# Load order, the order of a plain product's column halves, and the engine of the first block's remainders in a one-core decoder trunk kernel

## The chip, the cores and the metric

The kernel runs on one core of one Trainium2 chip. The core has TensorE (PE, matrix products, with the weight loads PEld beside them), VectorE (DVE), ScalarE (ACT), GpSimd (POOL) and SyncE (SP), which issues most of the transfers; each has an instruction queue of its own that it works through in order. The metric is the device time of one execution in microseconds, less is better. The kernel before takes 968.28 us, the median of three runs.

## What is computed

One layer of a decoder trunk over 1024 tokens and 16 meta tokens of width 1024. The root-mean-square norm of the tokens goes through one wide projection `w_in`, and its columns are shared out among four mixers (pooling, latent attention, a convolution module, a short gated convolution) and their gates; the four results are gated, projected, added, projected once more and normalised. This document is about the start only: the norm and the first columns of the projection.

```python
h = rms_norm(h_res, pre_norm_g[i])          # h_res: 16 meta tokens, then 1024 tokens
z = h @ w_in[i]
(pv, pg, cq, ckv, kr, mg, cu, cg, sbcx, sg, gl) = split_cols(z)
y_b = (mla_attention(cq, ckv, kr, ...) * jax.nn.silu(mg)) @ w_out_mla[i]
y_c = (conformer_conv(cu, ...) * jax.nn.silu(cg)) @ w_out_conf[i]
```

## The kernel before

**Precision.** Every fp32 operand of a product is kept as two parts, a rounded one ("hi") and the remainder ("lo"). A product is then three matmuls: hi by hi, hi weight by lo data, lo weight by hi data. `split` (line 497) makes the two: ACT copies the rounded part, another engine subtracts it from the source. Unless it is told otherwise that is POOL.

**Tokens and blocks.** The 1024 tokens are eight tiles of 128, x0 to x7. Transposed, with the 1024 rows of the projection in two halves, they make four blocks of data: B11 and B21 from x0 to x3 (first and second half of the rows), B12 and B22 from x4 to x7. The 16 meta tokens (`xm`) become columns 512 to 527 of B11 and B21. The projection is done with 7 products of sums and differences of blocks in place of 8. So there are four more operands: T1, T2, T4 from the differences of x tiles t and t + 4, and T3, which shares its buffer's name with B12. On the weights' side a block of 512 rows by 128 columns gives A11, A12, A22 and the sums S1 to S4. `prep` (line 592) loads two raw blocks, forms the sums on DVE and makes the seven pairs of hi and lo with `blk`. `unit` (line 633) runs the seven products for one range of columns of the tokens, into four PSUM banks.

**The plain product.** The columns `ckv` and `kr` (128 and 32 wide) are needed first and are not done with the sums. `plain` (line 678) runs, for one range of columns, four products of the raw weights: for the first half of the tokens (x0 to x3: `ckv` into bank pa, `kr` into pb), then for the second half (x4 to x7). It is called for the ranges U0 (columns 0 to 255, that is tiles 0, 1 and 4, 5) and U1 (columns 256 to 527: tiles 2, 3 and the meta tokens, and columns 256 to 511 of the second half: tiles 6, 7). All four need hi and lo of their data in both halves of the rows.

**One tile's way.** `load_x` issues the load on SP. `square` sums the squares (ACT, with a table function that accumulates), POOL forms the reciprocal root of the mean in two small instructions (`rsqrt_mean`, tile `rsx`), DVE multiplies the tile by it and by the gain (`scaled`, two halves of 512), PE transposes each half in four 128x128 pieces into a PSUM bank (`operand_of`, two banks x and one y in turn), ACT copies the rounded part, DVE subtracts to get the remainder. `parts` does this for the tiles that it is given, with one reciprocal root for all of them. `sums_of(t)` then forms four differences of tiles t and t + 4 on POOL, in place, and makes T1, T2 and T4 from them.

**What sets the order.** The program is not issued as written. A planner (`Plan`) records every operation, with an estimated length and its dependencies, and then emits each engine's operations in the order that its own clock gives. Operations inside `plan.ahead` come earlier than their place. When PE has nothing ready the planner puts in up to eight transposes of the identity in a row (tile `ps_w`), which nothing reads; they stop after the first block. Tiles come from small rings, so an operation may also wait for the buffer of an earlier one: the seven buffers `blk` hold x1 to x3, the meta tokens and the plain weights first, then the first block's weights.

**Order around the change.** The loads go out as x0, x1, x4, x5, the two raw blocks of the plain weights (`raw_kv`, 320 KB each), x2, x6, x3, x7, meta tokens; an x tile has 512 KB. The calls are `parts(0)`, `parts(1)`, the splits of the plain weights, `parts(4, 5)`, `parts(2, 6)`, `parts(3, 7)`, `meta()`, then `plain` for U0, the sums of tiles 0 and 1, `prep` of the first block, the sums of 2 and 3 and `plain` for U1.

Of the kernel before, what the change touches and what calls it, by code (L numbers as in the profile page):

```python
# [23 lines left out]
BF16 = mybir.dt.bfloat16  # L24
AF = mybir.ActivationFunctionType
ALU = mybir.AluOpType
# [4 lines left out]
P = 128  # L31
D = 1024
# [21 lines left out]
C_CU, C_CG, C_SC, C_SG, C_GL = 1440, 1952, 2208, 2976, 3232  # L54
# [8 lines left out]
B11, B21, B22, T1, T2, T3, T4 = range(7)  # L63

B12 = T3
# [6 lines left out]
def f(ap):  # L72
    return ap.bitcast(F32)
# [397 lines left out]
def trunk_kernel(ctx, tc, a):  # L471
    nc = tc.nc
    plan = Plan(nc)
    PE, ACT, DVE, POOL, SP = (plan.engine(e) for e in ("PE", "ACT", "DVE", "POOL", "SP"))
    ctx.enter_context(tc.manual_schedule())

    def pool(stack, grain=64, **kw):
        return plan.open(stack, Pool(plan, stack.enter_context(tc.tile_pool(bufs=1, **kw)), grain=grain,
                                     psum=kw.get("space") == PSUM,
                                     side="dram" if kw.get("space") == DRAM else kw.get("side", "left")))  # L480
# [4 lines left out]
    def copy(out, in_, scale=1.0):  # L485
        ACT.activation(out, in_, AF.Copy, scale=scale)

    def sub(eng, out, x, y):
        eng.tensor_tensor(out, x, y, op=ALU.subtract)

    def add(eng, out, x, y):
        eng.tensor_tensor(out, x, y, op=ALU.add)
# [4 lines left out]
    def split(hi, lo, src, eng=None):  # L497
        copy(hi, src)
        sub(eng or POOL, lo, src, f(hi))
# [12 lines left out]
    def rsqrt_mean(out, ssq, n, eps=EPS, eng=DVE):  # L512

        eng.tensor_scalar(out, ssq, 1.0 / n, eps, op0=ALU.mult, op1=ALU.add)
        POOL.tensor_tensor(out, out, mhalf[:out.shape[0], :out.shape[1]], op=ALU.pow)
# [43 lines left out]
    def bank(tag="x"):  # L559

        return psum.tile([P, 512], F32, tag=tag, bufs=2 if tag == "x" else 1, name=f"ps_{tag}")
# [3 lines left out]
    tp = pool(one, name="tp", reuse_waits="tile")  # L565
# [3 lines left out]
    def t4(shape, dt=F32, name="t4"):  # L569
        return tp.tile(shape, dt, tag="t4", bufs=4, name=name)  # L570
# [12 lines left out]
    def raw(name):  # L583

        return wp.tile([P, KH, 2 * P], F32, tag="raw", bufs=3, name=name)

    def blk(src, name):
        b = wp.tile([P, 2, KH, P], F32R, tag="blk", bufs=7, name=name)
        split(b[:, 0], b[:, 1], src)
        return b  # L590

    def prep(c):

        (a11, a21), (a12, a22) = ((t[:, :, :P], t[:, :, P:]) for t in (wload(0, c), wload(1, c)))
        ss = raw("ss")
        s1, s2 = ss[:, :, :P], ss[:, :, P:]
        add(DVE, s1, a21, a22)  # L600
        sub(DVE, s2, s1, a11)
        sub(DVE, a21, a11, a21)
        w = {n: blk(src, n) for n, src in (("A11", a11), ("S2", s2), ("S1", s1), ("S3", a21))}
        sub(DVE, s2, a12, s2)
        w.update({n: blk(src, n) for n, src in (("A12", a12), ("A22", a22), ("S4", s2))})
        return w

    def product(ps, w, b, c0, n, start, stop):
# [66 lines left out]
            out(0, 1, pc, u2[:, :nb], u2)  # L675
        pump()

    def plain(w, c0, n, out):

        for j, bs in enumerate(((B11, B21), (B12, B22))):  # L680
            for i, m in enumerate((P, 64)):
                ps = bank(("pa", "pb")[i])[:m, :n if j == 0 else min(n, 512 - c0)]
                for h, b in enumerate(bs):
                    (product, stacked)[i](ps, w[h][i], b, c0, n, h == 0, h == 1)
                with plan.ahead(EVAC):
                    out(i, j, ps, None, None)
# [35 lines left out]
    def out_raw(names, c0, n):  # L722

        z, place = pairs_of(n)

        def out(i, j, ps, x, tmp):
            second = i in z
            full(place(i, j, ps), x, ps)
            if second:
                store_both(names[i], z[i][:ps.shape[0]], c0, n)  # L730
        return out
# [60 lines left out]
    def wload(i, c, n=2 * P):  # L792

        t = raw("raw")
        for e, c_ in enumerate(c if isinstance(c, tuple) else (c,)):
            m = P if isinstance(c, tuple) else n
            SP.dma_start(t[:, :, P * e:P * e + m], w_in[:, KH * i:KH * (i + 1), c_:c_ + m])
        return t

    xt = {}  # L800

    def load_x(t):

        xt[t] = (t4([P, D], name="x") if t in (4, 5, 6, 7) else
                 wp.tile([P, D], F32, tag="raw", bufs=3, name="x") if t == 0 else
                 wp.tile([P, D], F32, tag="blk", bufs=7, name="x"))
        for c in (slice(0, 512), slice(512, D)) if t == 0 else (slice(0, D),):
            SP.dma_start(xt[t][:, c], a["x"][0, P * t:P * (t + 1), c])
    g8 = tp.tile([KD, P], F32, tag="wraw", bufs=2, name="g8")

    with plan.slow(-2000):
        load_x(0)
        ACT.dma_start(g8, a["pre_norm_g"][0].rearrange("(k p) -> k p", p=P))
        load_x(1)
        load_x(4)
        load_x(5)
        raw_kv = [wload(i, C_CKV, P + 32) for i in range(2)]
        for t in (2, 6, 3, 7):
            load_x(t)
        xm = wp.tile([NM, D], F32, tag="blk", bufs=7, name="xm")  # L820
        SP.dma_start(xm, a["meta_tokens"])
# [8 lines left out]
    ssx = const.tile([P, 16], F32, name="ssx")  # L830
    rsx = const.tile([P, 16], F32, name="rsx")

    def square(x_, t):
        n = x_.shape[0]
        ACT.activation(tp.tile([P, D], BF16, tag="whl", name="junk")[:n], x_, AF.Square, accum_out=ssx[:n, t:t + 1])

    def scaled(x_, t):
        n = x_.shape[0]
        for i in range(2):
            s = slice(512 * i, 512 * (i + 1))  # L840
            DVE.scalar_tensor_tensor(x_[:, s], x_[:, s], rsx[:n, t:t + 1], gB[i][:n], op0=ALU.mult, op1=ALU.mult)
# [3 lines left out]
    def operand_of(b, t, src):  # L845

        turn[0] += 1
        pt = bank("xxy"[turn[0] % 3])
        for k in range(KH):
            PE.transpose(pt[:, P * k:P * (k + 1)], src[:, P * k:P * (k + 1)], ident)  # L850
        p3 = pt.rearrange("p (k n) -> p k n", n=P)
        c = slice(P * t, P * (t + 1))
        copy(HB[b][:, 0, :, c], p3)
        sub(DVE, HB[b][:, 1, :, c], p3, f(HB[b][:, 0, :, c]))

    def parts(*ts):

        r0 = turn[1]
        turn[1] += len(ts)
        for i, t in enumerate(ts):  # L860
            square(xt[t], r0 + i)
        rsqrt_mean(rsx[:, r0:r0 + len(ts)], ssx[:, r0:r0 + len(ts)], D, eng=POOL)
        for i, t in enumerate(ts):
            scaled(xt[t], r0 + i)
            for j, b in enumerate(((B11, B21), (B12, B22))[t // 4]):
                operand_of(b, t % 4, xt[t][:, 512 * j:512 * (j + 1)])

    def sums_of(t):

        (b11, b21), (b12, b22) = ((xt[i][:, :512], xt[i][:, 512:]) for i in (t, t + 4))  # L870
        sub(POOL, b11, b12, b11)
        sub(POOL, b12, b22, b12)
        sub(POOL, b22, b22, b11)
        sub(POOL, b21, b21, b22)
        for b, src in ((T1, b11), (T2, b22), (T4, b21)):
            operand_of(b, t, src)

    def meta():
        square(xm, 8)
        rsqrt_mean(rsx[:NM, 8:9], ssx[:NM, 8:9], D, eng=POOL)  # L880
        scaled(xm, 8)
        pt = bank()
        for k in range(KD):
            PE.transpose(pt[:, NM * k:NM * (k + 1)], xm[:, P * k:P * (k + 1)], ident[:NM, :NM])
        b1, b2 = (pt[:, 64 * i:64 * (i + 1)].rearrange("p (k n) -> p k n", n=NM) for i in range(2))
        hm = up.tile([P, 2, KH, NM], F32, tag="u2", name="hm")
        copy(hm[:, 0], b1)
        sub(DVE, hm[:, 1], b2, hm[:, 0])
        for b, src, eng in ((B11, b1, DVE), (B21, b2, DVE), (T2, b1, DVE), (T4, hm[:, 1], DVE)):
            split(HB[b][:, 0, :, 512:LH], HB[b][:, 1, :, 512:LH], src, eng)  # L890
# [12 lines left out]
    U0, U1 = (0, 256), (256, 256 + NM)  # L903
# [6 lines left out]
    w_kv = [[blk(t[:, :, :P], "kv")] for t in raw_kv]  # L910
    kr = wp.tile([P, 2, KH, 64], F32R, tag="blk", bufs=7, name="kr")
    for i, t in enumerate(raw_kv):
        split(kr[:, i, :, :32], kr[:, i, :, 32:], t[:, :, P:P + 32])
        w_kv[i].append(kr[:, i])
    parts(4, 5)
    out_kv = [out_raw(("ckv", "kr"), *u) for u in (U0, U1)]
    parts(2, 6)
    parts(3, 7)
    meta()
    plain(w_kv, *U0, out_kv[0])  # L920
    for t in range(2):
        sums_of(t)
    w = prep((C_CU, C_CU + 256))
    for t in range(2):
        operand_of(T3, t, xt[t + 4][:, :512])
    for t in range(2, 4):
        sums_of(t)
    plain(w_kv, *U1, out_kv[1])
    for t in range(2, 4):
        operand_of(T3, t, xt[t + 4][:, :512])  # L930
    prow = w1([P, P], name="prow")
# [530 lines left out]
    for i, (_, names, kind) in enumerate(pairs):  # L1462
# [11 lines left out]
        w = nxt  # L1474
# [381 lines left out]
    for d in (0, 4, 1, 5, 2, 6, 3, 7):  # L1856
        whl = [wtile(ep, "w_out_mla", d, i) for i in range(2)]
        th = ep.tile([P, NT], F32, tag="th", bufs=3, name="th")
        ld(th, th_dram[8 + d])
        for c in range(2):  # L1860
            t = th[:, 512 * c:512 * (c + 1)]
            py = bank("u")
            for k in range(4):
                b = boM[c][k]
                w = whl[k // 2][:, :, k % 2]
# [154 lines left out]
```

## Time and profile before

| | before |
|---|---|
| median of three runs | 968.28 us (965.73 to 969.6) |
| the profiled execution | 959.63 us |
| its span, first to last instruction | 957.9 us |
| mean granted TensorE clock | 0.997 |
| data moved | 205.96 MB, mean 215 GB/s |
| instructions | 15219 |

The profiled execution has its own time; the span leaves out 1.7 us around the instructions. Nearly all instructions are recorded by one helper and carry line 361, so rows are told apart by their tiles: `ps_pa<-B,kv` is a matmul into bank pa of the operand B with the weights kv. In a timeline a row holds the start, the length, the engine, the operation, out<-in with sizes, how many of them follow one another, and in brackets the idle time before them with what ended it. PE's lengths overlap, since matmuls are pipelined; the distance between two starts is what a row occupies. The first 33 us, up to the meta tokens, are the stage in which the tiles are normalised and transposed; the first block's `unit` follows the plain product.

The fullest rows of what engines wait for in the first 60 us (waiter, waited for, us in total, times, longest):

```profile
POOL rsx L361 <- ACT junk L361: 7.6, 3, 4.0
DVE x L361 <- POOL rsx L361: 4.6, 3, 2.5
ACT z L361 <- DVE z L361: 4.1, 2, 3.6
DVE u L361 <- PE ps_pb L361: 3.7, 2, 2.5
ACT junk L361 <- DMA x<-in_x_dram: 3.0, 3, 1.5
```

### The profile page before, as it was taken

Reading aid. Unit: us, or ns where it says so; the run is one execution under the profiler, and the core shown is the slowest. Engines: PE = TensorE matmul, PEld = TensorE weight load, DVE = VectorE, ACT = ScalarE, POOL = GpSimd, SP = SyncE. Lnnn points to the kernel's source line nnn. Section 1 sums busy time; section 2 is a strip of 40 time slices with the busy share of each in tenths; the row PEclk is TensorE's granted clock in tenths of the full one; section 3 lists DMA queues with packets and bytes.
Section 4 is the critical chain, followed back from the end, with each engine's and each line's share of the span. In section 5 each row is a group of like instructions: output and inputs, shape, how many; then the busy total and the mean of one; then the engine's idle time right before and its main releaser. Section 6 shows DMA issues by size and latency. Waiting matters only on the chain.

```text
span 957.9 us, 15219 instructions
## 1 busy us (share of the span) xinstructions
PE 943.9 (99%) x4945; PEld 804.2 (84%) x4945; DVE 720.2 (75%) x1124; ACT 453.5 (47%) x925; POOL 677.7 (71%) x627
## 2 busy tenths in 40 slices
PE   8999999999999999999999999999999999999996
PEld 8998999988888888888888888888878878788885
DVE  6856979996999799547583657337778888799857
ACT  7752343434444445544454543266556565225632
POOL 5957669668787768669775977466467686738955
PEclk9999999999999999999999999999999999999998
DMA  8146566676779886788686678798978663783543
GB/s 262 46 126 198 151 202 196 211 224 204 249 229 280 281 283 209 244 224 245 221 255 187 191 243 279 220 300 259 294 207 275 199 184 111 264 266 107 189 141 144
DMA packets 143876, 205.96 MB, mean 215 GB/s; under 512 B 21169, under 2 KB 88752, under 8 KB 143028
## 3 DMA queue, kind: packets, MB, share of 16 engines
q1 hardware_dynamic: 134820, 188.20, 63.9%
q10 hardware_dynamic: 8656, 15.74, 4.5%
q8 instruction: 39, 0.64, 0.3%
q0 software_dynamic: 320, 1.05, 0.3%
q14 instruction: 41, 0.34, 0.1%
HBM read 132.01 MB, written 72.89 MB: 214 GB/s over the span
## 4 chain that ended last, share of the span: by engine, by line
PE 92%; DVE 3%; POOL 2%; issue 1%; ACT 1%; DMA 1%; SPq 0%; DVEq 0%; POOLq 0%; ACTq 0%
PE ps_pa L361 17%; PE ps_pb L361 17%; PE ps_pc L361 16%; PE ps_o L361 9%; PE ps_pd L361 8%; PE ps_u L361 7%; PE ps_s L361 7%; PE ps_y L361 6%; PE ps_x L361 4%; DMA x<-in_x_dram 1%; DVE th L361 1%; POOL pt L361 0%; ACT junk L361 0%; DVE op L361 0%; DVE c L361 0%
## 5 line engine op out<-in xcount | busy, mean ns | idle before, releaser
L361 PE MATMUL ps_pa<-B,A 128*128 128x512 f32 (+2 forms) x792 | 171.9, 359 | 0.0
L361 PE MATMUL ps_pb<-T,S 128*128 128x512 f32 (+2 forms) x792 | 170.7, 358 | 0.2 <-DVE u L361 0.2
L361 PEld LDWEIGHTS ps_pb<-T,S 128*128 128x128 f32 x792 | 134.4, 189 | 22.4 <-DVE u L361 0.4
L361 PEld LDWEIGHTS ps_pa<-B,A 128*128 128x128 f32 x792 | 134.2, 188 | 21.2 <-issue 0.2
L361 POOL TENSOR_TENSOR S<-ss,S 128x512 fp32r<-128x512 f32 x84 | 116.4, 1398 | 50.1 <-ACT S L361 43.3
L361 POOL TENSOR_TENSOR pt<-p,pt 128x512 fp32r<-128x512 f32 (+1 forms) x96 | 102.2, 1089 | 53.3 <-PE ps_s L361 27.4
L361 POOL TENSOR_TENSOR A<-raw,A 128x512 fp32r<-128x512 f32 x84 | 114.3, 1370 | 36.0 <-ACT A L361 35.7
L361 DVE TENSOR_TENSOR u<-ps_pb,u 128x512 f32<-128x512 f32 (+2 forms) x66 | 40.2, 610 | 67.3 <-PE ps_pb L361 62.2
L361 DVE SCALAR_TENSOR_TENSOR ps_w<-conv,par,ps_w 128x512 f32<-128x512 f32 x116 | 87.2, 752 | 2.5
L361 PE MATMUL ps_y<-bo,whl 128*128 128x512 f32 x288 | 84.6, 404 | 0.2 <-DVE th L361 0.2
L361 PE MATMUL ps_pd<-T,A 128*128 128x512 f32 (+2 forms) x396 | 84.5, 358 | 0.0
L361 PE MATMUL ps_pc<-T,S 128*128 128x512 f32 (+1 forms) x396 | 83.9, 357 | 0.0
L361 PE MATMUL ps_pc<-B,S 128*128 128x512 f32 (+1 forms) x396 | 83.7, 357 | 0.0
L361 ACT ACTIVATE S<-ss 128x512 fp32r<-128x512 f32 x84 | 50.2, 627 | 63.7 <-DVE ss L361 42.9
L361 ACT ACTIVATE p<-ps_s 128x512 f32<-128x512 f32 (+4 forms) x112 | 49.6, 444 | 61.2 <-PE ps_s L361 29.2
L361 PEld LDWEIGHTS ps_pd<-T,A 128*128 128x128 f32 x396 | 67.4, 188 | 10.9
L361 PEld LDWEIGHTS ps_pc<-B,S 128*128 128x128 f32 x396 | 66.9, 188 | 10.9
L361 PEld LDWEIGHTS ps_pc<-T,S 128*128 128x128 f32 x396 | 66.7, 189 | 11.0 <-issue 0.3
L361 PE MATMUL ps_o<-pt,vt 128*128 128x512 f32 (+7 forms) x288 | 68.9, 347 | 0.6 <-ACT ol L361 0.5
L361 PE MATMUL ps_s<-qt,kt 100*128 100x512 f32 (+4 forms) x336 | 68.7, 324 | 0.5 <-ACT p L361 0.5
L361 DVE TENSOR_TENSOR z<-ps_pc,u 128x512 f32<-128x512 f32 (+1 forms) x64 | 38.8, 606 | 33.9 <-PE ps_pc L361 27.4
L361 PEld LDWEIGHTS ps_s<-qt,kt 100*128 100x128 f32 (+1 forms) x336 | 54.1, 176 | 10.2 <-DVE qt L361 0.7
(298 smaller groups left out, 1924.7 us busy)
## 6 DMA issues: line engine op xcount, KB each, us to landing
raw<-in_w_in_dram SPq DMA_DIRECT2D x52, 512.0 KB
th<-th SPq DMA_DIRECT2D x32, 512.0 KB
th<-z ACTq DMA_DIRECT2D x60, 256.0 KB
v<-vhl SPq DMA_DIRECT2D x16, 384.0 KB
vt<-v SPq DMA_DIRECT2D x8, 768.0 KB
qt<-q SPq DMA_DIRECT2D x16, 384.0 KB
bo<-bo SPq DMA_DIRECT2D x6, 1024.0 KB
w_out_mla<-whl SPq DMA_DIRECT2D x16, 256.0 KB
```

The lines of the kernel that those rows point to most:

```text
L361: getattr(self.handle[o["eng"]], o["op"])(*map(real, o["args"]), **{k: real(v) for k, v in o["kw"].items()})
```

## The change

The loads now go out as x0, x1, the plain weights, x4, x5, x6, x7, x2, x3. `parts` takes the tiles as 4 alone (its sum of squares on DVE, as a product of the tile with itself that accumulates), 5 alone, 6 with 7, 2 with 3. `plain` for U1 does the second half of the tokens first. In `prep` of the first block the remainders alternate between POOL and DVE (A11, S1, A12, S4 on POOL; S2, S3, A22 on DVE). No matmul is added or left out; the planner orders the whole program anew.

```diff
-    def blk(src, name):
+    def blk(src, name, eng=None):
         b = wp.tile([P, 2, KH, P], F32R, tag="blk", bufs=7, name=name)
-        split(b[:, 0], b[:, 1], src)
+        split(b[:, 0], b[:, 1], src, eng)
         return b
 
-    def prep(c):
+    def prep(c, engs=(None, None)):
...
-        w = {n: blk(src, n) for n, src in (("A11", a11), ("S2", s2), ("S1", s1), ("S3", a21))}
+        w = {n: blk(src, n, engs[i % 2]) for i, (n, src) in enumerate((("A11", a11), ("S2", s2), ("S1", s1), ("S3", a21)))}
         sub(DVE, s2, a12, s2)
-        w.update({n: blk(src, n) for n, src in (("A12", a12), ("A22", a22), ("S4", s2))})
+        w.update({n: blk(src, n, engs[i % 2]) for i, (n, src) in enumerate((("A12", a12), ("A22", a22), ("S4", s2)))})
         return w
...
-    def plain(w, c0, n, out):
-
-        for j, bs in enumerate(((B11, B21), (B12, B22))):
+    def plain(w, c0, n, out, order=(0, 1)):
+
+        for j in order:
+            bs = ((B11, B21), (B12, B22))[j]
...
         load_x(1)
-        load_x(4)
-        load_x(5)
         raw_kv = [wload(i, C_CKV, P + 32) for i in range(2)]
-        for t in (2, 6, 3, 7):
+        for t in (4, 5, 6, 7, 2, 3):
             load_x(t)
...
-    def square(x_, t):
+    def square(x_, t, eng=ACT):
         n = x_.shape[0]
-        ACT.activation(tp.tile([P, D], BF16, tag="whl", name="junk")[:n], x_, AF.Square, accum_out=ssx[:n, t:t + 1])
+        junk, s = tp.tile([P, D], BF16, tag="whl", name="junk")[:n], ssx[:n, t:t + 1]
+        if eng is DVE:
+            DVE.scalar_tensor_tensor(junk, x_, 1.0, x_, op0=ALU.mult, op1=ALU.mult, accum_out=s)
+        else:
+            ACT.activation(junk, x_, AF.Square, accum_out=s)
...
-    parts(4, 5)
+    parts(4, eng=DVE)
+    parts(5)
     out_kv = [out_raw(("ckv", "kr"), *u) for u in (U0, U1)]
-    parts(2, 6)
-    parts(3, 7)
+    parts(6, 7)
+    parts(2, 3)
     meta()
     plain(w_kv, *U0, out_kv[0])
     for t in range(2):
         sums_of(t)
-    w = prep((C_CU, C_CU + 256))
+    w = prep((C_CU, C_CU + 256), (POOL, DVE))
...
-    plain(w_kv, *U1, out_kv[1])
+    plain(w_kv, *U1, out_kv[1], (1, 0))
```

More of the change, by code (lines that the diff above doesn't have):

```diff
@@ L854, in operand_of, with parts @@
         sub(DVE, HB[b][:, 1, :, c], p3, f(HB[b][:, 0, :, c]))
-    def parts(*ts):
+    def parts(*ts, eng=ACT):
         r0 = turn[1]
@@ L860, in parts @@
         for i, t in enumerate(ts):
-            square(xt[t], r0 + i)
+            square(xt[t], r0 + i, eng)
         rsqrt_mean(rsx[:, r0:r0 + len(ts)], ssx[:, r0:r0 + len(ts)], D, eng=POOL)
```

## The prediction

> **What bounds the kernel now.** First the busy shares, then the table of stretches, with a cut at each place where the program's phase changes. Columns of the second: stretch, its length, busy time and instructions of PE, PEld, DVE, ACT and POOL, granted clock, DMA share, GB/s.
>
> ```profile
> PE 943.9 (99%) x4945; PEld 804.2 (84%) x4945; DVE 720.2 (75%) x1124; ACT 453.5 (47%) x925; POOL 677.7 (71%) x627
> ```
>
> ```profile
> 0.00:11.50 11.50, 9.23 (x57) 8.41 (x58) 3.79 (x8) 7.13 (x13) 3.00 (x16) 1.00 0.85 288
> 11.50:33.00 21.50, 20.45 (x175) 19.31 (x174) 19.15 (x30) 17.20 (x38) 19.53 (x22) 1.00 0.50 157
> 33.00:60.00 27.00, 27.00 (x230) 26.85 (x231) 18.31 (x30) 15.98 (x34) 19.40 (x16) 1.00 0.34 102
> 60.00:900.00 840.00, 837.88 (x4261) 708.48 (x4260) 640.18 (x998) 396.53 (x803) 598.95 (x545) 1.00 0.72 223
> 900.00:958.00 58.00, 49.37 (x230) 41.17 (x228) 38.75 (x60) 16.66 (x39) 36.78 (x31) 0.95 0.45 159
> ```
>
> ```profile
> PE 92%; DVE 3%; POOL 2%; issue 1%; ACT 1%; DMA 1%; SPq 0%; DVEq 0%; POOLq 0%; ACTq 0%
> ```
>
> TensorE is the bound: from 60 to 900 us it idles 2.12 us of 840, and the chain of work that ended last is 92% PE. The change leaves the useful matmuls as they are and gives the last units the same order, so it can pay only where PE idles or runs idle-time transposes that feed nothing. Those fillers (tile ps_w) count as busy, so the PE share hides them. This is the row of their group between 11.5 and 33.1 us (count, busy us, mean ns), and then PE's timeline where most of them stand (start, length, operation, idle before):
>
> ```profile
> L361 PE MATMUL ps_w<-ident 128*128 128x128 f32 x33 | 5.0, 276 | 0.0
> ```
>
> ```profile
> 27.59 0.60 PE L361 MATMUL ps_w<-ident 128*128 128x128 f32 x4
> 28.02 0.60 PE L361 MATMUL ps_x<-ident,x 128*128 128x128 f32 x4
> 28.46 0.71 PE L361 MATMUL ps_w<-ident 128*128 128x128 f32 x5
> 29.00 0.60 PE L361 MATMUL ps_y<-ident,x 128*128 128x128 f32 x4
> 29.44 0.38 PE L361 MATMUL ps_w<-ident 128*128 128x128 f32 x2
> 29.66 0.60 PE L361 MATMUL ps_x<-ident,x 128*128 128x128 f32 x4
> 30.10 0.82 PE L361 MATMUL ps_w<-ident 128*128 128x128 f32 x6
> 30.84 0.42 PE L361 MATMUL ps_x<-ident,xm 16*128 16x16 f32 x4
> 31.19 0.44 PE L361 MATMUL ps_w<-ident 128*128 128x128 f32 x2
> ...
> 33.04 0.60 PE L361 MATMUL ps_x<-ident,x 128*128 128x128 f32 x4
> ```
>
> Lengths overlap in the pipeline, so a price is a distance of starts: four fillers take 28.02 - 27.59 = 0.43 us, 0.109 each; four 16-wide ones 31.19 - 30.84 = 0.35. From 27.59 to 33.04 are 5.45 us. In them stand 20 fillers (2.18), 12 transposes of x (1.31) and 8 of the meta tokens (0.70). The rest, 1.26 us, is idle. So 3.44 us of this stretch feed nothing. It ends when the meta tokens' columns are ready, because the next product (columns 256 to 527) needs them.
>
> **The change, part by part.** *1. Plain weights third in the load order, x4's sum of squares on DVE.* ACT now, with the idle time and its releaser in brackets:
>
> ```profile
> 6.83 1.06 ACT L361 ACTIVATE junk<-x 128x1024 bf16<-128x1024 f32 x1 [1.34 <-DMA x<-in_x_dram]
> 8.16 1.06 ACT L361 ACTIVATE junk<-x 128x1024 bf16<-128x1024 f32 x1 [0.18 <-DMA x<-in_x_dram]
> 9.22 0.58 ACT L361 ACTIVATE B<-ps_x 128x512 fp32r<-128x512 f32 x1
> 10.73 0.58 ACT L361 ACTIVATE B<-ps_y 128x512 fp32r<-128x512 f32 x1
> 12.18 1.15 ACT L361 ACTIVATE kv<-raw 128x512 fp32r<-128x512 f32 x2
> ```
>
> Tiles land 8.16 - 6.83 = 1.33 us apart. The weights were there by 12.18, since nothing is waited for in front of that row. With two tiles fewer ahead they are there by 12.18 - 2.66 = 9.5, and not before x1 (6.83). The first half will be about 8.3. ACT's first weight copy stands ahead of x0's two copies (9.22, 10.73). At 8.3 these come at about 8.9 and 9.4, no later than now; at 9.5 the first comes 0.9 later, of which the matmuls behind still hide half. x4 and x5 come some 1.7 us later (640 KB at 512 KB in 1.33), x6 takes x2's place and x2, x3 the last ones. SP issues the loads in that order, well ahead of the transfers, which reach x1 only at 6.8; the two weight loads' issues are two places earlier than in this row:
>
> ```profile
> 3.07 1.73 SPq L361 DMA_DIRECT2D raw<-in_w_in_dram  x2
> ```
>
> On DVE stands the new square:
>
> ```order
> L361 TENSOR_TENSOR B11_239<-ps_x_227,B11_239 128x4x128
> L361 TENSOR_TENSOR B21_262<-ps_y_237,B21_262 128x4x128
> L361 TENSOR_TENSOR B11_239<-ps_x_249,B11_239 128x4x128
> L361 TENSOR_TENSOR B21_262<-ps_x_264,B21_262 128x4x128
> L361 SCALAR_TENSOR_TENSOR x_168<-x_168,rsx_212,ps_pc_187 128x512
> ```
>
> Above: DVE before, the remainders of x0 and x1 for the operands B11 and B21, then the scaling of x4. Below: DVE of the changed program at the same place.
>
> ```order
> L361 TENSOR_TENSOR B11_238<-ps_x_223,B11_238 128x4x128
> L361 TENSOR_TENSOR B21_248<-ps_y_235,B21_248 128x4x128
> L361 SCALAR_TENSOR_TENSOR junk_274,ssx_200<-x_172 128x1024
> L361 TENSOR_TENSOR B11_238<-ps_x_246,B11_238 128x4x128
> L361 TENSOR_TENSOR B21_248<-ps_x_266,B21_248 128x4x128
> L361 SCALAR_TENSOR_TENSOR x_172<-x_172,rsx_212,ps_pc_187 128x512
> ```
>
> The square stands ahead of x1's remainders, and the second matmul of the first plain product reads the first of them. No row of before has a 1024-wide DVE square. The nearest are operations with two SBUF sources (the tile view gives least/median/most ns, the group row a mean):
>
> ```profile
> L361 DVE SCALAR_TENSOR_TENSOR z<-z x4: 424/554/841, 59.1 to 71.2; 128x256 f32<-128x256 f32 x3, 128x272 f32<-128x272 f32 x1
> L361 DVE TENSOR_TENSOR z<-ps_pc,u x4: 424/424/426, 57.2 to 70.7; 128x256 f32<-128x256 f32 x4
> L361 DVE SCALAR_TENSOR_TENSOR z<-u,z 128x512 f32<-128x512 f32 x10 | 13.8, 1381 | 1.2 <-ACT u L361 1.2
> L361 DVE TENSOR_TENSOR B<-ps_x,B 128x512 fp32r<-128x512 f32 x9 | 6.0, 683 | 0.1
> ```
>
> From 256 to 512 elements costs 683 - 424 = 259 ns, so 1024 undisturbed are 0.42 + 3 x 0.26 = 1.2 us. Twice the 512-wide mean, with POOL busy, is 2.8. I take 1.2, because POOL has its large weight splits behind it by then. DVE's second remainder now starts at 11.35 after 0.41 of waiting for ACT; freed of that it ends near 11.5, so the square ends near 12.7 and x1's first remainder near 13.4:
>
> ```profile
> 11.35 0.69 DVE L361 TENSOR_TENSOR B<-ps_y,B 128x512 fp32r<-128x512 f32 x1 [0.41 <-ACT B L361]
> 11.49 1.04 PE L361 MATMUL ps_w<-ident 128*128 128x128 f32 x8
> 12.86 0.51 PE L361 MATMUL ps_pa<-B,kv 128*128 128x256 f32 x2 [0.34 <-ACT kv L361]
> ```
>
> PE leaves the common part at 11.49, runs 14 fillers where it ran 13 (1.53 us) and two first matmuls (0.25), and asks at 13.3. Terms: one filler more, +0.11; the wait of 0.34 gone; a wait of 0.1 to 0.7 in its place, I take 0.3.
>
> [...]
>
> *2. Second column half first.* PE before, around the meta tokens (x_147 and x_216 are x tiles, xm the meta tokens, ps_w the fillers):
>
> ```order
> L361 MATMUL ps_w_139<-ident_62 128x128 x5
> L361 MATMUL ps_y_529<-ident_62,x_147 128x128 x4
> L361 MATMUL ps_w_139<-ident_62 128x128 x2
> L361 MATMUL ps_x_538<-ident_62,x_216 128x128 x4
> L361 MATMUL ps_w_139<-ident_62 128x128 x6
> L361 MATMUL ps_x_555<-ident_62,xm_220 128x16 x4
> L361 MATMUL ps_w_139<-ident_62 128x128 x2
> ```
>
> PE of the changed program there (kv and kr are the plain weights, T3 and B22 the operand of x4 to x7):
>
> ```order
> L361 MATMUL ps_x_543<-ident_62,x_216 128x128 x4
> L361 MATMUL ps_pa_512<-B22_364,kv_258 128x256 x2
> L361 MATMUL ps_y_551<-ident_62,x_147 128x128 x4
> L361 MATMUL ps_pa_512<-B22_364,kv_258 128x256 x7
> L361 MATMUL ps_pb_569<-T3_357,kr_277 64x256
> L361 MATMUL ps_x_571<-ident_62,xm_227 128x16 x4
> L361 MATMUL ps_pb_569<-T3_357,kr_277 32x256
> ```
>
> The plain product's last 256 columns over x4 to x7, which needs no meta tokens, has moved into the gap. Of the 20 fillers two remain: -18 x 0.109 = -1.96. The idle 1.26 goes, as the meta tokens have work on both sides. What is late next: PE comes to tiles x6, x7 and x2 as DVE scales them, and DVE waits for POOL's reciprocal root, 19.98 - 18.97 = 1.01 us from its start:
>
> ```profile
> 18.97 0.19 POOL L361 TENSOR_SCALAR rsx<-ssx 128x2 f32<-128x2 f32 x1
> 19.98 0.75 DVE L361 SCALAR_TENSOR_TENSOR x<-x,rsx,ps_pc 128x512 f32<-128x512 f32 x1 [1.01 <-POOL rsx L361]
> ```
>
> POOL takes it in order behind differences of 1.33 us, and the changed program has one such turn more (x4 and x5 apart). PE has other products between, so I charge 0.4 (0 to 1.0).
>
> *3. Remainders of the first block on two engines.* Three of seven go to DVE, from rows like these on POOL:
>
> ```profile
> 36.29 6.61 POOL L361 TENSOR_TENSOR x<-x 128x512 f32<-128x512 f32 x4
> 42.87 1.28 POOL L361 TENSOR_TENSOR S<-ss,S 128x512 fp32r<-128x512 f32 x1
> 44.12 0.72 POOL L361 TENSOR_TENSOR whl<-wraw,whl 128x256 fp32r<-128x256 f32 x1
> 44.81 1.75 POOL L361 TENSOR_TENSOR S<-ss,S 128x512 fp32r<-128x512 f32 x1
> ```
>
> And the first block's first product on PE, its last one, and what follows it:
>
> ```profile
> 48.04 0.63 PE L361 MATMUL ps_pa<-B,A 128*128 128x256 f32 x4
> 57.97 1.60 PE L361 MATMUL ps_pc<-B,S 128*128 128x256 f32 x12
> 59.41 1.67 PE L361 MATMUL ps_pa<-B,A 128*128 128x272 f32 x12
> ```
>
> POOL sheds 3 x 1.28 = 3.8 us; DVE gains 3 x 0.68 = 2.0, up to three times that beside POOL, and has 27 - 18.31 = 8.7 us idle from 33 to 60. PE has no idle time there, so nothing is won directly; it lets the first block keep up with a PE that comes 2.8 us earlier. Behind DVE's new splits stand the remainders that free PE's transpose banks; their cover is the 12 matmuls of each product (59.41 - 57.97 = 1.44 us). I take 0, with 2.6 as the bad end (below).
>
> **Sum:** +0.11 - 0.34 + 0.3 - 1.96 - 1.26 + 0.4 = **-2.75 us**. The profiled execution took 959.63 (span 957.9 and 1.7 around it), so 956.9. It lies 8.65 below the median of the three runs (968.28); I carry the difference over: **965.5**, and with the smaller terms' ends 964.8 to 966.8.
>
> **Rivals.** *A, the square is slow* (2.8 us, POOL holding DVE off): 1.6 us more at PE's second matmul, and all behind it: 967.1. For it: the 841 ns beside POOL; against: POOL then has only short work. *B, the wait moves to the first block.* POOL's 16 differences still start when x4 is scaled, near 16 us, and still end near 42.5. The changed program then has two small splits (0.72 and less) and the S1 remainder (1.3 to 1.75), done near 45 to 46, and the A12 remainder next, 46 to 47.5. PE enters the block at 48.04 - 2.75, less four groups of transposes that now come later (4 x 0.44), so near 43.5; behind it two products and one such group (3.3) stand ahead of S1 and A12, which it wants near 47. It may wait 1.3 for A12's and another 1.3 if the differences stretch as in the row of 6.61 (four at 1.33 are 5.3): 2.6 lost, 968.1, no change. *C, slower: the turns through POOL.* If each of three turns (x4, x6 with x7, x2 with x3) finds POOL inside a difference, it costs DVE 1.01 + 1.33 = 2.34, 7.0 in all, where DVE now waits 1.0 for them. 6.0 more against 3.15 (the gain without my 0.4) is 2.85 slower: 971.1. It decides when DVE's idle time from 11.5 to 33 us, now 21.5 - 19.15 = 2.35, passes 5.5. Against it: PE has products in reserve between the tiles. *D, the weights don't come earlier*: bounded above, at most 0.5: inside the forecast.
>
> **How the numbers follow.** Forecast 0.57, A 0.13, B 0.20, C 0.08, a larger gain 0.02. No case but the tail of C reaches 4.8 us, 0.5% of the median and about what a measurement of this kernel can tell from no change. The three runs spread 965.73 to 969.6, two either way, which gives the forecast's far end a chance to pass it: faster 0.12, same 0.82, slower 0.06. Range: 964.8 less 2 is 962.8; B's 968.1 plus 1.5 is 969.6.
>
> **What would show it.** Right: some 16 fillers from 11.5 us on, none between 25 us and the first block; the meta tokens' transposes without idle time before them; the first block's last product, with columns 0 to 255, ending near 56.7 instead of 59.4; from there every product 2.75 us earlier. A: a DVE square over 2 us, followed by a PE wait of over 1. B: PE waits for POOL or DVE on A12 or S1 near 47. C: several waits of DVE for rsx over 2 us. I am wrong altogether if stages after 60 us gain or lose over 2 us, which nothing in the rows suggests.

## The result, and the profile after

| | before | after |
|---|---|---|
| median of 20 runs, taken side by side | 967.98 us | 964.89 us |
| ratio, with its 95% interval | | 0.9956 (0.9937 to 0.9975) |
| the profiled execution | 959.63 us | 965.38 us |
| its span | 957.9 us | 963.6 us |
| mean granted TensorE clock | 0.997 | 0.994 |

The median fell by 3.1 us to 964.89; 965.5 was forecast. (One of the changed kernel's twenty runs was disturbed, at 1163.61 us; the ratio, of the means of all other runs, leaves it out.) But the profiled execution of the changed kernel took 5.7 us *more* than that of before. Both are true, so the first thing to do with these traces is to find the places where the difference between them changes.

First the busy shares of the changed kernel, the shares of its chain of waits, and its table of stretches with the cuts that were used for before.

```profile
PE 946.0 (98%) x4928; PEld 803.0 (83%) x4928; DVE 726.0 (75%) x1129; ACT 449.9 (47%) x923; POOL 677.5 (70%) x626
```

```profile
PE 87%; DVE 4%; issue 3%; POOL 2%; DMA 2%; ACT 1%; SPq 1%; DVEq 0%; ACTq 0%; POOLq 0%
```

```profile
11.50:33.00 21.50, 21.34 (x184) 20.79 (x185) 20.23 (x32) 17.09 (x38) 19.48 (x24) 1.00 0.54 163
33.00:60.00 27.00, 26.98 (x229) 26.30 (x227) 22.56 (x36) 17.06 (x39) 16.41 (x15) 1.00 0.36 114
60.00:900.00 840.00, 833.81 (x4215) 702.24 (x4215) 638.02 (x991) 388.70 (x792) 594.67 (x540) 1.00 0.71 222
```

From 11.5 to 33 us PE idles 0.16 us where it idled 1.05. From 60 to 900 it idles 6.19 where it idled 2.12: the head of the program became denser, and something far behind it became worse. The share of the chain that is PE fell from 92% to 87%, DVE's and "issue" grew.

**The head.** The group of the fillers between 11.5 and 33.1 us, and PE's timeline of the changed kernel from its last fillers to the meta tokens:

```profile
L361 PE MATMUL ps_w<-ident 128*128 128x128 f32 x16 | 2.3, 272 | 0.0
```

```profile
20.96 0.38 PE L361 MATMUL ps_w<-ident 128*128 128x128 f32 x2
...
32.15 0.28 PE L361 MATMUL ps_pb<-T,kr 128*64 128x256 f32 x1
32.35 0.41 PE L361 MATMUL ps_x<-ident,xm 16*128 16x16 f32 x4
32.70 0.55 PE L361 MATMUL ps_pb<-T,kr 128*32 128x256 f32 x3
33.08 0.60 PE L361 MATMUL ps_x<-ident,x 128*128 128x128 f32 x4
33.44 0.48 PE L361 MATMUL ps_pb<-T,kr 128*64 128x256 f32 x2
33.85 0.41 PE L361 MATMUL ps_x<-ident,xm 16*128 16x16 f32 x4
```

16 fillers instead of 33, the last at 20.96, and the meta tokens' transposes with products on both sides and no idle time. The first block's end, as it was announced:

```profile
43.72 0.40 PE L361 MATMUL ps_pa<-B,A 128*128 128x256 f32 x2
...
55.39 1.60 PE L361 MATMUL ps_pc<-B,S 128*128 128x256 f32 x12
56.83 1.42 PE L361 MATMUL ps_pa<-B,A 128*128 128x272 f32 x10
```

The product behind the block starts at 56.83; it started at 59.41. That is 2.58 us, against 2.75 forecast.

**Behind the head.** Three marks that both programs have, at the same place of PE's work: the first product of 512 columns of the third unit, the first product of attention, and the third transpose of row maxima in attention (the fourth of a tile `mr`, and so called in the expectations below). Before and after:

```profile
72.59 2.66 PE L361 MATMUL ps_pb<-T,S 128*128 128x512 f32 x11
...
629.38 2.92 PE L361 MATMUL ps_s<-qt,kt 100*128 100x512 f32 x17
...
660.41 0.27 PE L361 MATMUL ps_s<-ident,mr 128*4 128x128 f32 x1
```

```profile
70.00 2.88 PE L361 MATMUL ps_pb<-T,S 128*128 128x512 f32 x12
...
627.85 3.15 PE L361 MATMUL ps_s<-qt,kt 100*128 100x512 f32 x18
...
659.77 0.27 PE L361 MATMUL ps_s<-ident,mr 128*4 128x128 f32 x1
```

2.59 us ahead at the first mark, 1.53 at the second, 0.64 at the third. No wait is long enough to show it: from 72 to 629 us the trace names a single wait of PE in either run, 0.2 and 0.3 us. Then the difference stays at 0.63 until 737 us, and there it turns round at one instruction. DVE, POOL and PE of the changed kernel:

```profile
733.71 6.74 POOL L361 TENSOR_TENSOR pt<-p,pt 128x512 fp32r<-128x512 f32 x6
```

```profile
735.42 5.57 DVE L361 TENSOR_TENSOR m<-m,th 128x512 f32<-128x512 f32 x1
```

```profile
737.56 0.63 PE L361 MATMUL ps_y<-bo,whl 128*128 128x512 f32 x2
741.98 0.64 PE L361 MATMUL ps_s<-kt,qt 96*128 96x328 f32 x1 [3.79 <-DVE qt L361]
...
742.84 1.48 PE L361 MATMUL ps_o<-pt,vt 128*128 128x512 f32 x3
```

A sum of 512 elements on DVE, which the change does not touch, takes 5.57 us here and 1.37 in the trace of before. PE waits 3.79 us behind it, and its next matmuls are slow: three of 512 columns take 1.48 where the same three take 0.85 in a run without the stall. 5.7 us behind is where the profiled run stays to its end.

### The profile page after: what moved, and what is told of

Read it like the earlier page. It is cut to its first block, busy times and chain, and to the rows that moved or that the text cites. A ratio compares the mean times of both kernels' runs of the same rounds, so it can differ in the third digit from the quotient of the medians.

```text
span 963.6 us, 15185 instructions
## 1 busy us (share of the span) xinstructions
PE 946.0 (98%) x4928; PEld 803.0 (83%) x4928; DVE 726.0 (75%) x1129; ACT 449.9 (47%) x923; POOL 677.5 (70%) x626
## 3 DMA queue, kind: packets, MB, share of 16 engines
q0 software_dynamic: 320, 1.05, 0.3%
## 4 chain that ended last, share of the span: by engine, by line
PE 87%; DVE 4%; issue 3%; POOL 2%; DMA 2%; ACT 1%; SPq 1%; DVEq 0%; ACTq 0%; POOLq 0%
PE ps_pa L361 16%; PE ps_pb L361 16%; PE ps_pc L361 15%; PE ps_o L361 9%; PE ps_pd L361 7%; PE ps_u L361 7%; PE ps_s L361 7%; PE ps_y L361 6%; PE ps_x L361 4%; DMA kt<-kr 1%; DMA vs<-v 1%; DVE th L361 1%; SPq L361 1%; DMA x<-in_x_dram 1%; POOL pt L361 1%
## 5 line engine op out<-in xcount | busy, mean ns | idle before, releaser
L361 POOL TENSOR_TENSOR S<-ss,S 128x512 fp32r<-128x512 f32 x83 | 114.4, 1391 | 70.6 <-ACT S L361 70.4
L361 PEld LDWEIGHTS ps_y<-bo,whl 128*128 128x128 f32 x288 | 51.3, 189 | 9.3 <-DVE th L361 0.9
```

Of the source, the lines that this page charges most:

```text
L361: getattr(self.handle[o["eng"]], o["op"])(*map(real, o["args"]), **{k: real(v) for k, v in o["kw"].items()})
```

## The experiments

They ran in four groups, each group on one chip, beside the kernel before on that chip. "Mark" is the first of the three above. x1's tile lands when DMA delivers it, which varies; ACT's square of x1 starts at 6.12 to 7.63 us in the fourteen traces, whatever the load order, and moves the mark by some tenths.

**1. The column halves in the old order.**

```diff
-    plain(w_kv, *U1, out_kv[1], (1, 0))
+    plain(w_kv, *U1, out_kv[1])
```

> The changed kernel with the column halves of the second plain product in the old order (columns 256 to 527 first). The mark is the start of the third unit's first pb product of 512 columns: 72.59 us before, 70.00 in the changed kernel. Theory (the second half first carries the gain): PE's program has 22 fillers more (69 against 47), 22 x 0.109 = 2.4 us, and waits for the meta tokens again, so the mark is at 72.4 to 73.6. Rival (load order and two engines carry it): mark at 70.0 to 70.6.

Mark at 73.03: the theory. 38 fillers in the window of the row above, 16 in the changed kernel. And at all three marks this run is 0.44, 0.50 and 0.50 us behind before: PE's order from 64 us on, still in the first blocks, is matmul by matmul that of before, and a difference made in the head is carried through unchanged. Median 960.86 us against 960.52, ratio 1.000 (0.999 to 1.0009). So the load order, the square on DVE and the two engines bring nothing without the halves' order.

**2. x4's sum of squares on ACT.**

```diff
-    parts(4, eng=DVE)
+    parts(4)
```

> The changed kernel with x4's sum of squares on ACT again, still by itself. Theory (the DVE square of 1.42 us pays, since ACT's squares land after the plain weights' copies): 8 fillers more (55 against 47) are 0.87 us, and PE's wait of 0.28 at its second plain matmul goes: mark at 70.4 to 70.8. Rival (the square on DVE costs more than it gives): mark at 69.4 to 69.8.

Mark at 71.52, worse than either case. The fillers were counted rightly (8 more). Not foreseen is PE's wait in front of a transpose at 27.59 us:

```profile
PE ps_x L361 <- DVE T L361: 0.6, 1, 0.6
PE ps_x L361 <- ACT hm L361: 0.3, 1, 0.3
```

The square on DVE is worth 1.5 us with this order of the halves. Median 962.33, ratio 1.0019 (1.0002 to 1.0035). Three of its ten runs are over 963.5, and the profiled one (963.96) shows the stall of 735 us at another place, a product on DVE that begins just inside a row of POOL:

```profile
759.40 3.80 POOL L361 TENSOR_TENSOR pt<-p,pt 128x512 fp32r<-128x512 f32 x3
```

```profile
759.60 4.15 DVE L361 TENSOR_TENSOR op<-ol,rb 64x512 f32<-64x512 f32 x1
```

The shortest of the twelve products of this kind takes 0.68 us. PE then waits 1.08 and 1.30 us. So the stall is not tied to the one sum.

**3. All remainders of the first block on POOL.**

```diff
-    w = prep((C_CU, C_CU + 256), (POOL, DVE))
+    w = prep((C_CU, C_CU + 256))
```

> The changed kernel with all remainders of the first block on POOL again. Theory (part 3 buys nothing as POOL ends in time; nothing was waited for in the changed kernel): mark at 69.9 to 70.3. Rival (part 3 is what let the first block keep up): PE waits for S1's and A12's remainders near 47 us, 0.6 to 2.6 in all, mark at 70.6 to 72.6.

Mark at 70.09, and PE waits for nothing from 11 to 60 us: part 3 buys nothing. Here, too, the lead shrinks, 2.50, 1.39, 0.50 at the three marks. Median 961.96, ratio 1.0008 (0.9996 to 1.0019).

**4. The halves' order alone**, in the kernel before.

```diff
-        for j, bs in enumerate(((B11, B21), (B12, B22))):
+        for j in order:
+            bs = ((B11, B21), (B12, B22))[j]
...
-    plain(w_kv, *U1, out_kv[1])
+    plain(w_kv, *U1, out_kv[1], (1, 0))
```

> The kernel before with the second column half first and nothing else of the change. Theory (the halves' order works by itself, but x6 and x7 arrive alternating with x2 and x3, so T3 and B22 are ready later): 9 fillers fewer than before (55 against 64), 1.0 us, and up to 1.26 us of idle time less: mark at 70.4 to 71.6. Rival (it needs the load order): mark at 72.3 or later; rival (load order adds nothing): 70.0.

Mark at 72.13, a gain of 0.46, which is between the two cases. The fillers went as counted, but x1's square starts at 7.63 here, 0.80 later than in the trace of before. The three traces of the changed kernel pass such a delay on nearly whole (square at 7.05, 7.38, 7.60; mark at 69.74, 70.00, 70.22). An estimate from these is that it hides 0.7 us here, so that the halves' order alone is worth about 1.2, within the theory. That is less than half of the 2.59 of the whole change. What nobody expected is the end: median 985.47, ratio 1.0254 (1.0239 to 1.0269), 25 us slower with a head that is half a microsecond faster. SP's queue and what it waits for from 595 to 652 us, then PE:

```profile
615.84 2.42 SPq L361 DMA_DIRECT2D so<-in_w_o_dram  x2
631.15 4.67 SPq L361 DMA_DIRECT2D so<-so  x4
635.92 0.38 SPq L361 DMA_DIRECT2D qt<-q  x1
...
644.62 1.29 SPq L361 DMA_DIRECT2D vs<-v  x3
```

```profile
SPq L361 <- DVE so L361: 15.6, 4, 12.8
```

```profile
648.72 3.91 PE L361 MATMUL ps_s<-qt,kt 100*128 100x512 f32 x15 [18.92 <-DMA vs<-v]
```

The planner put the preparation of the output weights (tile `so`) later in this program. In SP's queue attention's loads, from 635.92 on, stood behind stores that waited for DVE, one of them 12.8 us, and PE stood 18.92 us behind the loads. In the kernel before those stores were issued by 601.6 us. Behind the wait PE's clock is at half until 657.67, 8.95 us, which costs another 4.5 by an estimate from these numbers; with the wait that is 23.4 of the 25. (The mean granted clock of this execution is 0.986; in experiment 1, on the same chip, it is 0.998.) The planner answers a shift of a microsecond in the head with another order 600 us further on.

**5. The changed kernel again, twice, on other chips.**

> The changed kernel once more, unchanged, beside the kernel before on one chip. Theory (the head's 2.6 us have shrunk to 0.6 by 660 us, and one DVE sum, m<-m,th near 735 us, takes 1.4 or 5.6 us by chance, as DVE and POOL reach for the same SBUF operands' path): runs in two groups, 958.5 to 961 and 964 to 967; against runs of before without such a stall (959.7 to 961) the lower group is 0.3 to 1.0 us faster, ratio 0.999 to 1.003 by how many fall in the upper one. Rival (the change's gain of 2.6 to 4.3 us is real to the end): ratio 0.9955 to 0.9975 again, with all runs at 956.5 to 958.5.

Median 959.57 against 960.63, ratio 0.9987 (0.9968 to 1.0005). 11 of 12 runs lie at 958.8 to 962.2, one at 966.0. The marks are 2.85 and 1.32 us ahead, then 0.53 behind: in this execution PE also waited for the first gate weights, a transfer that was in time before.

```profile
643.21 0.47 PE L361 MATMUL ps_y<-bo,whl 128*128 128x512 f32 x1 [0.63 <-DMA whl<-w_out_pool]
```

And the sum that took 5.57 us, with POOL's row beside it; PE's wait behind it is gone:

```profile
734.87 7.24 POOL L361 TENSOR_TENSOR pt<-p,pt 128x512 fp32r<-128x512 f32 x6
```

```profile
736.60 1.38 DVE L361 TENSOR_TENSOR m<-m,th 128x512 f32<-128x512 f32 x1
```

The program is the same. POOL's six subtractions take 7.24 us instead of 6.74: here the third of them takes 1.75 us where it took 1.29, and DVE's sum was done at 737.98, with POOL's row going on to 742.11; in the other execution it was not done before the row was.

> The changed kernel a third time, unchanged, beside before on one chip, to count how often the tail stalls and how early attention begins. Theory: the third unit's mark is 2.5 to 2.9 us earlier than before's 72.59, the first attention product 1.2 to 1.6 earlier than before's 629.38, the fourth transpose of row maxima (before 660.41) between 0.7 earlier and 0.6 later, by how the first gate weights' transfer falls; ratio 0.997 to 1.000 by runs without a stall. Rival (the first measurement's 0.9956 holds on any chip): 0.9937 to 0.9975 and every mark 2.5 earlier.

Median 965.11 against 966.28, ratio 0.9962 (0.9934 to 0.999). Five runs at 958.7 to 959.4, seven at 964.8 to 968.0, none between. The profiled run is one of the seven, and the same sum shows 5.57 us again, with 3.79 of waiting on PE. Marks: 2.37 and 1.28 ahead, 0.51 behind. How often a run is over 963.5 us differs from chip to chip: 11 of 19 runs in the first comparison, 1 of 12 and 7 of 12 in these, and of before's runs beside them 18 of 20, 3 of 35 and 22 of 27. That before's long runs have the same stall is not shown, since its one trace is of a run of 959.63. Their granted clock points the same way: on these two chips 0.992 to 0.996 over 963.5, and 0.996 to 0.998 below.

**6. The gate's product left in PSUM**, so that DVE's sum has one SBUF operand: in the changed kernel, and in before.

```diff
-                        DVE.scalar_tensor_tensor(t, t, 1.0, py, op0=ALU.add, op1=ALU.mult)
-                        add(POOL if bi == 1 and c else DVE, m_[c][d], m_[c][d], t)
+                        pool = bi == 1 and c
+                        g = t if pool else py
+                        DVE.scalar_tensor_tensor(g, t, 1.0, py, op0=ALU.add, op1=ALU.mult)
+                        add(POOL if pool else DVE, m_[c][d], m_[c][d], g)
```

> The changed kernel with the gate's product left in its PSUM bank, so that DVE's sum into m reads one operand from SBUF and one from PSUM. Theory (DVE's sums with two SBUF operands are held off while POOL runs its back-to-back splits): every such sum takes 0.66 to 0.72 us, none over 1; the upper group of 964 to 967 is gone; median 958 to 961, 0.3 to 2 us below the changed kernel's lower group at best. Rival (the 5.57 us are not the operands' doing): a sum of over 1 us remains near 735, and the two groups remain.

> The kernel before with the same edit in the gate alone. Theory: all those sums at 0.66 to 0.72 us (mean 0.95 before), DVE 8 us less busy after 700; median 0.5 to 2.5 us below before's on the same chip, as PE waited little for those sums. Rival (the order the scheduler makes of it decides): within 0.5 us of before or slower.

The sums of the changed kernel so edited (least, median, most ns), and what PE waited for from 795 us on:

```profile
L361 DVE TENSOR_TENSOR m<-m,ps_y x24: 616/686/689, 721.3 to 831.1; 128x512 f32<-128x512 f32 x24
```

```profile
PE ps_y L361 <- DVE m L361: 1.3, 2, 0.9
```

None of the 24 sums takes over 0.69 us beside the same work of POOL: it is the second operand in SBUF that makes a sum wait. Of the 24 runs of the two kernels one lies over 963.5 (at 963.64), which says little, as the changed kernel has one in 12 on this chip. The gain does not come: medians 961.51 and 962.19 against 960.63 of before (1.0004, 0.9988 to 1.002; 1.0006, 0.9992 to 1.0021). The bank that the product stays in comes free later, and PE waits 1.3 us for it in the last branch, in both kernels; without the edit it waits 0.2 there.

**7. x4 loaded ahead of the plain weights.**

```diff
+        load_x(4)
         raw_kv = [wload(i, C_CKV, P + 32) for i in range(2)]
-        for t in (4, 5, 6, 7, 2, 3):
+        for t in (5, 6, 7, 2, 3):
```

> The changed kernel with x4 loaded ahead of the plain weights instead of behind them. Theory (x1 landed 0.55 us later because the weights' transfers run beside it): x1's square is back at 6.83 us (7.38 in the changed kernel), 44 fillers against 47, and the third unit's mark at 69.2 to 69.8 instead of 70.00. Rival (x1's landing depends on something else): the square stays at 7.2 to 7.5; or the weights now come too late and the mark is at 70.2 to 71.0.

x1's square at 7.41: nothing speaks for the theory that x1 is late because of the transfer behind it, though one trace of a landing that scatters this much is weak evidence. ACT now waits 0.7 us for the weights and the mark is at 70.85, as the second rival said. Median 962.43, ratio 1.0011 (0.9991 to 1.0032).

**8. Fewer sums through PSUM**, eight (second branch, first half), then the one that stalled. The diffs show the line that decides; the sum reads `g` as above.

```diff
+                        g = py if bi == 1 and not c else t
```

> The changed kernel with the gate's product left in PSUM for eight sums alone: those of the second branch's first half, one of which is the sum that took 5.57 us. Theory (two SBUF operands make it wait for POOL; the bank held longer costs little here, as PE's 1.3 us of waits for ps_y in the wider edit lay in the last branch): those eight sums at 0.66 to 0.72 us, no run over 963.5, median 0 to 1 us below the changed kernel on the same chip. Rival (any new order of attention loses a microsecond or two, as in the wider edit): median 960.5 to 962.5.

```diff
+                        g = py if (bi, d, c) == (1, 2, 0) else t
```

> The changed kernel with the gate's product left in PSUM for one sum alone, the one that took 1.4 or 5.6 us near 735 (second branch, third weight tile, first half). Theory (that one wait for POOL makes the upper group, and the order up to there is the changed kernel's own): this sum at 0.66 to 0.72 us, at most 2 of 12 runs over 963.5, the other runs at 958.5 to 961.5. Rival (as with eight sums, the new order behind it costs 1 to 3 us, or another sum or product with two SBUF operands takes the stall over): the lowest run over 960, or a group at 964 to 967 as before.

With eight: 961.78 against 966.28 of before, ratio 0.9953 (0.9933 to 0.9973), on the chip on which the changed kernel stalled in 7 of 12 runs; here 1 of 11 is over 963.5, and the lowest run is 960.67, against 958.7 of the changed kernel. So 3.3 us better in the median there, with a floor 2 us higher, as the rival said. In its trace another sum with two SBUF operands takes 3.54 us, at 788.05. With one sum:

```profile
736.60 0.69 DVE L361 TENSOR_TENSOR m<-m,ps_y 128x512 f32<-128x512 f32 x1
```

960.12 against 961.34, ratio 0.9981 (0.9967 to 0.9996), 12 of 12 runs under 963.5 (lowest 959.26) where before had 6 of 17 over it. Each of the two ended below before on its own chip; which of them, or of the changed kernel, is best over all chips no run decides, since they ran on different ones, and the changed kernel as it stands did not run on that of the one sum.

**9. The gate products that fill attention begin four units later.**

```diff
-        while count["f"] < min(48, 48 * count["u"] / (NUNIT - 2)):
+        while count["f"] < min(48, 48 * (count["u"] - 4) / (NUNIT - 6)):
```

> The changed kernel with the gate products that fill attention beginning four of its 112 units later. Theory (attention's entry gives back part of the gain, since PE comes 1.5 us earlier to loads that do not come earlier: in the second run of the changed kernel PE waited 0.63 us there for the first gate weights): no PE wait for a DMA from 628 to 661 us, the first attention product 1.2 to 1.6 earlier than before's 629.38 and the fourth transpose of row maxima 1.0 to 1.6 earlier than before's 660.41 by equal work (the order of fills differs, so up to 2 us more by position), median 0.3 to 1.2 us below the changed kernel on the same chip. Rival (the loss at the entry is not the loads'; or the fills are missed there): median equal or up to 2 us above.

No wait for a transfer from 628 to 662 us, and the third mark is 1.32 ahead, after 2.11 at the second (x1 landed early in this execution), with as many matmuls of each shape done as in the changed kernel. The lead still shrinks by 0.79 at the entry, and two of the changed kernel's three traces have no such wait either, so that the moved fills helped there is not shown. The products that were put off are missed later:

```profile
PE ps_y L361 <- DVE th L361: 2.4, 4, 1.5
```

Median 962.68, against 965.11 of the changed kernel on that chip, but its lowest run is 961.73, 3 us above that kernel's. So the rival's second half is what the trace shows.

## Why the prediction was right, and where not

**Fillers, -1.96, and idle time, -1.26: right.** 17 fillers fewer (18 off, one more at the start), and no idle time at the meta tokens. Experiment 1 puts both back and loses 3.03 us, the largest effect of any part. (The 1.26 is worked out from distances of starts. The idle time that the tables show for 11.5 to 33 us fell by 0.89, from 1.05 to 0.16, with the wait for ACT in it.)

**The wait for ACT, -0.34, and the square on DVE, +0.3: right.** DVE and PE of the changed kernel:

```profile
12.00 1.42 DVE L361 SCALAR_TENSOR_TENSOR junk<-x 128x1024 bf16<-128x1024 f32 x1
13.35 0.08 DVE L361 DVE_READ_ACCUMULATOR junk<-x 128x1 f32 x1
13.35 1.28 DVE L361 TENSOR_TENSOR B<-ps_x,B 128x512 fp32r<-128x512 f32 x2
```

```profile
13.47 0.49 PE L361 MATMUL ps_w<-ident 128*128 128x128 f32 x3
14.08 1.81 PE L361 MATMUL ps_pa<-B,kv 128*128 128x256 f32 x13
```

1.42 us where 1.2 was taken; the last fillers end their turn at 13.47 + 3 x 0.109 = 13.80 and PE starts at 14.08, a wait of 0.28. The square took 1.22 to 2.19 us in the nine other traces that have it on DVE, all inside the bounds of 1.2 and 2.8, so rival A falls for this trace. It is nearest in the three with x1's square at 6.55 or earlier (experiment 6 in the changed kernel, 8 with eight sums, 9): there the square takes 1.79 to 2.19 us beside POOL's last weight splits, and PE waits 0.6 to 1.0 us for one of those.

**Turns through POOL, +0.4: too much, by little.** DVE waits for rsx 1.0 us from 11.5 to 33, as before, in two waits instead of one, and PE waits for none of it. Rival C falls. So does rival D: ACT copies the first half of the plain weights at 8.44 us without waiting for them, where it copied them at 12.18.

**Remainders on two engines, 0: right,** by experiment 3. Rival B falls: PE takes the first S1 product at 47.03 and the first A12 product at 47.15 without a wait.

**x1's landing: missed, 0.55 us.** x1's square started at 7.38 instead of 6.83. In the fourteen traces it scatters with either load order. By the three traces of the changed kernel (experiment 4) this cost the head some 0.5 us. With the 0.4 that was charged for POOL and not paid, it is why the head's 2.58 us came so near to 2.75: two misses that nearly cancel.

**The step that failed: "from there every product 2.75 us earlier",** and "I am wrong altogether if stages after 60 us gain or lose over 2 us, which nothing in the rows suggests". They lost 1.95, 3.38 and 2.88 us from the first to the third mark in the three traces of the changed kernel. What the runs show in its place has three parts.

- *From the first mark to attention*, 1.06 to 1.53 us. Most of it lies between 127 and 338 us by the clock of before. There PE runs the same 1194 matmuls (as many of each tile and shape) in 210.81 us before (210.85 and 210.88 in the two programs that kept before's order there), and in 211.94 to 211.97 in the three traces of the changed kernel, in another order. The programs of experiments 2, 3, 6 (changed kernel), 8 and 9 lose 1.07 to 1.32 there, that of experiment 7 3.78 (1.9 of it one wait for ACT); the two whose PE order up to attention is that of before, experiment 1 (behind the head) and the second of 6, lose nothing. So it goes with the other order in which the planner interleaves the small products. It is not a wait: PE's idle time among the 1194 is 0.24 us before and 0.30 after. Why the same products stand further apart in the new order stays open.
- *At the entry of attention*, 0.89 to 1.85 us. In the second trace, which loses 1.85, 0.63 of it is a wait for the first gate weights' transfer; PE comes earlier, the transfer does not. But the third trace loses 1.79 without such a wait, 0.35 of it in a wait for ACT. The rest is not attributed.
- *Near 735 us*, 6.3 and 5.6 us in the two traces in which DVE's sum stands behind POOL: 3.79 of waiting in each, the rest mostly slow matmuls behind it. The change does not touch that sum, and the stall decides what is measured; whether the change makes it rarer no run shows. On the chip where few runs are over 963.5 us, the difference is 1.1 us (959.57 against 960.63, the interval takes in no change). In the first comparison most runs of both kernels are over it, more of before's than of the changed kernel's, and the median moved by 3.1.

One more step has no row behind it: "It lies 8.65 below the median of the three runs (968.28); I carry the difference over". That took what separates the profiled execution from the median for something that both kernels have alike. Without it the sum says 956.9, and no run of the changed kernel in the three comparisons is that short: the lowest of its 44 is 958.70, and 959.37 is the lowest of before's 82.

So the forecast of 965.5 met 964.89 with a head of the right size, a loss behind it that it denied, and a stall that it did not know. The sum was right for the head and is not what the median measured; that the two agree so well is luck.

## What to carry to other kernels

A gain in the head of a planned program is worth what is left of it at the end: put marks at the same work in both traces, every hundred microseconds or so, and read how the lead changes, before the median is believed. Where a planner orders everything anew, a part of a change tried alone can cost ten times its own effect (experiment 4), so look at the order of the queue that issues the loads, and what its head waits for. And where one engine runs a row of back-to-back operations from SBUF, a two-operand operation of its neighbour inside that row may be held until the row ends: here DVE's sum took 5.57 us beside POOL's six subtractions, and 0.69 with one operand in PSUM.

## What the hardware did that was not expected

**DVE is held off by POOL for several instructions, not one.** The sum started 1.7 us into POOL's row of subtractions (735.42 against 733.71) and ended 0.54 after the row did (740.99 against 740.45); the shortest of the 40 sums of this kind in the trace of before takes 0.68. It was held for some 4.9 us while POOL, with six operations in 6.74 us, went from one to the next. In another execution of the same program it took 1.38. With one of its two operands in PSUM it took 0.69 (experiment 10). So here a sum with both operands in SBUF contended with POOL's subtractions, and for more than one of them: it waited for the rest of one and for four more. What the two engines share there, which the expectation ahead of experiment 5's first run calls a path, no trace shows.

**A wait of 3.79 us costs more than itself.** PE's granted clock in the stretches around it, and in the same work of the run without the stall:

```profile
738.00:742.00 4.00, 0.21 (x2) 0.03 (x1) 3.97 (x4) 0.69 (x2) 2.45 (x3) 0.77 0.73 172
742.00:748.00 6.00, 6.00 (x19) 4.91 (x20) 2.42 (x8) 1.50 (x6) 1.98 (x3) 0.59 0.17 44
748.00:755.00 7.00, 7.00 (x45) 6.23 (x44) 5.51 (x14) 3.74 (x11) 3.78 (x5) 1.00 0.44 153
```

```profile
739.00:745.00 6.00, 6.00 (x35) 5.30 (x34) 4.44 (x12) 4.75 (x13) 5.84 (x8) 1.00 0.73 155
```

0.59 of the clock for 6 us behind the wait, 19 recorded matmuls in place of 35. The clock is at half from 740.15 to 746.97 here (6.82 us), from 743.31 to 746.72 in the third trace of the changed kernel, and from 766.07 to 769.48 in that of experiment 2 (3.41 us each). The mean granted clocks of these executions are 0.994, 0.995 and 0.996; of the one without the stall 0.997. The clock fell 2.0 us into the wait here, and in experiment 2 in the second of two waits of 1.08 and 1.30 us. Behind the two waits of 3.79 us PE worked for 5.0 and 3.6 us before it was whole again, behind the one of 18.92 (experiment 4) for 8.95. Single waits of 1.9 (experiment 7) and 1.50 us (experiment 9) left it whole, and so did those of 0.6 us, which cost only themselves. What makes the clock fall after one wait and not after another these traces do not show.
